# Latent attention: side weights' load and rounding written apart, O's second bank read by one copy, sums over keys in one VectorE instruction

## The chip, the core and the metric

The kernel runs on one NeuronCore of a Trainium2 chip. The metric is the device time of one execution in microseconds (us), the median of several runs. The five engines are called as the profile calls them: PE (TensorE, matmuls; PEld its weight loads), DVE (VectorE), ACT (ScalarE), POOL (GpSimd) and SP (SyncE, which here issues the DMAs). PE writes to PSUM, eight banks of 128 x 512 float32; DVE and ACT read PSUM, POOL works on SBUF alone.

## The reference, cut to what matters

Two layers run over 2048 latent tokens and 256 context tokens. The first layer mixes a windowed attention (mixer A) and a latent attention (mixer B); the second is a neighbourhood attention (mixer C). The change lies in mixer B's attention, and in the loading of the output weights beside mixers B and C. Mixer B has 8 heads; each latent query reads all 2304 keys, each context query the 256 context keys:

```python
def mla_dense(qn, qr, kn, kr, v):
    scale = (B_NOPE + B_ROPE) ** -0.5
    s = (jnp.einsum('bqhd,bkhd->bhqk', qn, kn) + jnp.einsum('bqhr,bkr->bhqk', qr, kr)).astype(jnp.float32) * scale
    p = jax.nn.softmax(s, axis=-1).astype(v.dtype)
    return jnp.einsum('bhqk,bkhd->bqhd', p, v)
...
    y = jnp.concatenate([oa * jax.nn.silu(za), ob * jax.nn.silu(zb)], axis=-1) @ out_w
```

## The kernel before, in words

**Numbers in two parts.** A float32 value x is kept as a high part (x rounded to the matmul's format) and a low part (x minus the high part). A product of two such values takes three matmuls, high x high, high x low and low x high. A weight tile is loaded into `ws` (L252), rounded on ACT into `wh` (L254), and the low part `wl` is made on POOL (L255); `wprep` does all three.

**Mixer B, `attn_b`.** The work of a head is cut into chunks of queries, 512 wide (256 wide for the context and for head 0's first two), in the order context, 0, 512, 1024, 1536. Inside a chunk the loop runs over 18 tiles of 128 keys (2 for the context). One step of it, `score(j)`, makes the scores of a key tile in PSUM (`bs`, three matmuls, L959 to L961), the exponential's high part (ACT, L964), the exponential in place (ACT, L965), the low part `bpl` (DVE, L966), and adds the high part into `bacc` (POOL, L970), which holds the sums over keys, one value for each partition and query. `pv(j)` comes four steps later (`LAG`) and adds two matmuls into two banks: `o` (L979, high part) and `o2` (L980, low part, 65 columns: 64 of the output and one of row sums). Both banks exist once (`op`, one buffer for each), so the next chunk's first `pv` writes to them when the last chunk's values have been read.

**The handover, `fin`.** After the last `pv` of a chunk, ACT copies `o` to `bos` (L984); DVE adds the 64 rows of `o2` to it (L986) and adds row 64 of `o2` into row 64 of `bacc` (L987). Two DMAs store `bos` (L989).

**The denominators, `den`.** Seven steps after `fin` (`DLAG`), PE transposes `bacc` by four blocks of 128 x 128 into one PSUM bank (L995), and ACT copies each block with an accumulator (L999), which sums over the keys. The bank (`xp`, one buffer) is shared with the transposes of row maxima (L935).

**The row maxima.** Between the steps of one chunk, the row maxima of the next one are made by a high x high matmul (`bm`, L923) and a maximum on DVE (L925); two banks.

**The side weights.** While mixer B runs, the first seven of eight row blocks of the output weights are prepared (`out_weights`, two `wprep` calls for each block, three `wst` buffers). In heads 1 to 7 one block is written ahead of the chunk that begins at 1024, under `tc.issue_after(self.vdma)`: what the block issues on SP stands behind the last DMA of the newest head load (`load(h + 1)`, written at chunk 512, some 4.7 MB). In mixer C (`attn_c`, 64 units of four row groups) three blocks are written, at units 19, 23 and 27, with no such order.

**What sets the order.** In `attn_b` PE runs in the order in which the program is written (`manual_schedule`). The orders of ACT, DVE, POOL and SP are made when the program is built, by a planner that plays the whole program through a timeline (`schedule_with_timeline_sim=True`): for each engine it takes, among the instructions whose inputs and buffers are ready in its timeline, the one written first. On the chip each engine then runs its list strictly in order, and waits on semaphores.

Of the kernel before, what the change touches and what calls it, by code (L numbers as in the profile page):

```python
# [8 lines left out]
F32 = mybir.dt.float32  # L9
R32 = mybir.dt.float32r  # L10
BF16 = mybir.dt.bfloat16
AF = mybir.ActivationFunctionType
ALU = mybir.AluOpType
AX = mybir.AxisListType
PSUM = bass.MemoryType.PSUM

P = 128
# [83 lines left out]
class Kern:  # L101
# [145 lines left out]

    def wprep(self, rings, sp, src, w, name, eng=None, bufs=3):

        nc = self.nc  # L250
        s = sp.tile([P, 512], F32, tag="wst", bufs=bufs, name="ws" + name)
        self.wdma = nc.sync.dma_start(s[:, :w], src).ins  # L252
        h, l = [r.tile([P, 512], R32, name=f"w{x}{name}") for x, r in zip("hl", rings)]
        nc.scalar.activation(h[:, :w], s[:, :w], AF.Copy)  # L254
        (eng or nc.gpsimd).tensor_sub(l[:, :w], s[:, :w], f(h[:, :w]))  # L255
        return h, l
# [580 lines left out]
    def out_weights(self, l, k0, k1, rings):  # L837
# [3 lines left out]
                                      512, f"o{l}{k}{hf}") for hf in range(2)])  # L841
        return [lambda k=k: go(k) for k in range(k0, k1)]

    def attn_b(self):


# [2 lines left out]
        nc, tc, i, scr = self.nc, self.tc, self.i, self.scr  # L849
        with ExitStack() as ctx:  # L850
# [96 lines left out]
            def st_pieces(h, t0, n):  # L947
                t = H[h]
                c = t0 // P
                kts = list(range(NT)) if t0 < TL else [NTL, NTL + 1]  # L950
                st = {}

                def score(j):
                    kt = kts[j]
                    if j == 0:
                        st["acc"] = p1.tile([P, 512], F32, tag="acc", bufs=3, name=f"bacc{h}_{c}")
                    ps = sp.tile([P, 512], F32, tag="s", name=f"bs{h}_{c}_{j}")
                    ks, qs = slice(kt * P, (kt + 1) * P), slice(t0, t0 + n)
                    nc.tensor.matmul(ps[:, :n], t["kh"][0:97, ks], t["qh"][0:97, qs], start=True, stop=False)  # L959
                    nc.tensor.matmul(ps[:, :n], t["kh"][0:96, ks], t["ql"][0:96, qs], start=False, stop=False)  # L960
                    nc.tensor.matmul(ps[:, :n], t["kl"][0:96, ks], t["qh"][0:96, qs], start=False, stop=True)  # L961
                    hi = ph.tile([P, 512], R32, name=f"bph{h}_{c}_{j}")
                    lo = pl_.tile([P, 512], R32, name=f"bpl{h}_{c}_{j}")
                    nc.scalar.activation(hi[:, :n], ps[:, :n], AF.Exp)  # L964
                    nc.scalar.activation(ps[:, :n], ps[:, :n], AF.Exp)  # L965
                    nc.vector.tensor_sub(lo[:, :n], ps[:, :n], f(hi[:, :n]))  # L966
                    if j == 0:
                        st["h0"] = hi
                    else:
                        nc.gpsimd.tensor_add(st["acc"][:, :n], f((st["h0"] if j == 1 else st["acc"])[:, :n]), f(hi[:, :n]))  # L970
                    st[j] = (hi, lo)

                def pv(j):
                    if j == 0:
                        st["o"] = op.tile([P, 512], F32, tag="o", name=f"bo{h}_{c}")
                        st["o2"] = op.tile([P, 512], F32, tag="o2", name=f"bo2{h}_{c}")
                    hi, lo = st.pop(j)
                    fi, la = j == 0, j == len(kts) - 1
                    nc.tensor.matmul(st["o"][:, :n], t["v"][:, kts[j], 0:P], hi[:, :n], start=fi, stop=la)  # L979
                    nc.tensor.matmul(st["o2"][0:65, :n], t["v"][:, kts[j], 64 : P + 1], lo[:, :n], start=fi, stop=la)  # L980

                def fin():
                    o = p.tile([P, 512], F32, tag="os", name=f"bos{h}_{c}")
                    nc.scalar.activation(o[:, :n], st["o"][:, :n], AF.Copy)  # L984
                    acc = st["acc"]
                    nc.vector.tensor_add(o[0:64, :n], st["o2"][0:64, :n], o[0:64, :n])  # L986
                    nc.vector.tensor_add(acc[64:65, :n], st["o2"][64:65, :n], acc[64:65, :n])  # L987
                    for e in range(2):
                        nc.sync.dma_start(scr["o0"][e, 512 + h * 64 : 576 + h * 64, t0 : t0 + n], o[e * 64 : e * 64 + 64, :n])  # L989

                def den():
                    d, c0 = den_of(h, t0)
                    ps = xp.tile([P, 512], F32, tag="x", name=f"bdt{h}_{c}")
                    for x in range(n // P):
                        nc.tensor.transpose(ps[:, x * P : (x + 1) * P], st["acc"][:, x * P : (x + 1) * P], self.ident)  # L995
                    for x in range(n // P):
                        col = t0 // P + x - c0
                        j = p.tile([P, P], BF16, tag="dj", bufs=1, name=f"bdj{h}_{c}_{x}")
                        nc.scalar.activation(j, ps[:, x * P : (x + 1) * P], AF.Copy, accum_out=d[:, col : col + 1])  # L999
                    late.put(8, lambda: den_done(h, t0, n))  # L1000

                k = range(len(kts))
                return [lambda j=j: score(j) for j in k], [lambda j=j: pv(j) for j in k], fin, den
# [5 lines left out]
            DLAG = 7  # L1009
            load(0)  # L1010

            side = self.out_weights(0, 0, self.nw, self.wor)
            late = Later()

            size = [sum(NT if t0 < TL else 2 for t0, _ in ch) for _, ch in units]
# [23 lines left out]
            for h, ch in units:  # L1039
                if ch[0][0] == 512 and h + 1 < 8:  # L1040
                    load(h + 1)
                if h > 0 and ch[0][0] == 1024 and side:
                    with tc.issue_after(self.vdma):
                        side.pop(0)()
                for x in ch:
                    score, pv, fin, den = st_pieces(h, *x)
                    for j in range(len(score)):
                        pvs.append(pv[j])
                        run(score[j], pvs.pop(0) if len(pvs) > LAG else None)
                    late.put(LAG, fin)  # L1050
                    late.put(LAG + DLAG, den)
# [301 lines left out]
    def attn_c(self):  # L1353
# [5 lines left out]
        with ExitStack() as ctx:  # L1359
# [163 lines left out]
            for n, (h, cb) in enumerate(units):  # L1523
                if cb == 2 and h + 1 < 16:
                    load(h + 1)
                if n + 3 < len(units):
                    load_v(*units[n + 3])
                if n + 1 < len(units):
                    make_bias(*units[n + 1])
                if n == 16:  # L1530
                    side = self.out_weights(1, 0, self.nw, self.wor)
                if n % 4 == 3 and side:
                    side.pop(0)()
                sl, Pt = s_pieces(h, cb)
                if len(queue) < 2:
                    merge(sl, [])
                else:
                    emit_t(sl)
                queue.append((h, cb, Pt))
# [122 lines left out]
```

## Time and profile before

| | us |
|---|---|
| median of 3 runs | 3759.67 (3757.97 to 3761.63) |
| the profiled execution | 3758.57 |
| its span, first to last instruction | 3756.8 |
| PE busy in the span | 3507.8 (93%) |
| DVE, ACT, POOL busy | 2311.3, 1945.0, 1668.9 |
| mixer B's loop, first to last score matmul | 961.8 to 1999.3 |
| mixer C's loop, the same | 3010.2 to 3524.8 |

The time of an execution is its span and some 1.8 us around it. In the profile each engine's instructions have a start and a length, and idle time ahead of an instruction is put down to what ended it. Matmuls overlap in the pipeline: at full speed those of 512 columns start 0.23 us apart though each is shown with 0.39 us. Neighbours on ACT, DVE and POOL overlap a little too, so that spacing is read from start to start. PEclk is the TensorE clock that was granted, as a share of 2.4 GHz: 1.00 or 0.50 (1.2 GHz).

### The profile page before, as it was taken

Reading aid. Unit: us, or ns where it says so; the run is one execution under the profiler, and the core shown is the slowest. Engines: PE = TensorE matmul, PEld = TensorE weight load, DVE = VectorE, ACT = ScalarE, POOL = GpSimd, SP = SyncE. Lnnn points to the kernel's source line nnn. Section 1 sums busy time; section 2 is a strip of 40 time slices with the busy share of each in tenths; the row PEclk is TensorE's granted clock in tenths of the full one; section 3 lists DMA queues with packets and bytes.
Section 4 is the critical chain, followed back from the end, with each engine's and each line's share of the span. In section 5 each row is a group of like instructions: output and inputs, shape, how many; then the busy total and the mean of one; then the engine's idle time right before and its main releaser. Section 6 shows DMA issues by size and latency. Waiting matters only on the chain.

```text
span 3756.8 us, 53300 instructions
## 1 busy us (share of the span) xinstructions
PE 3507.8 (93%) x17607; PEld 2889.5 (77%) x17607; DVE 2311.3 (62%) x4313; ACT 1945.0 (52%) x4096; POOL 1668.9 (44%) x1573
## 2 busy tenths in 40 slices
PE   6999899999989888988989989999999999999888
PEld 5777778889767666766767867888788789999766
DVE  6445542499978777877886874212211088888665
ACT  4343332599767666766763123223221188888511
POOL 6555642211567666766774244223211243333432
PEclk8999999999999999999989999999999999999999
DMA  6767563852321222023027956554434476666686
GB/s 216 222 205 242 183 176 119 278 130 57 70 67 23 53 66 67 9 67 75 22 65 223 318 195 190 169 145 126 136 129 127 149 278 243 236 240 232 190 225 177
DMA packets 381054, 576.79 MB, mean 154 GB/s; under 512 B 35393, under 2 KB 218081, under 8 KB 370913
## 3 DMA queue, kind: packets, MB, share of 16 engines
q1 hardware_dynamic: 380777, 573.39, 50.1%
q8 instruction: 138, 2.26, 0.2%
q14 instruction: 139, 1.14, 0.1%
HBM read 399.36 MB, written 173.90 MB: 153 GB/s over the span
## 4 chain that ended last, share of the span: by engine, by line
PE 66%; DMA 14%; DVE 7%; issue 5%; POOL 4%; ACT 3%; SPq 2%; POOLq 0%; ACTq 0%; DVEq 0%
PE mm L263 7%; PE mm L262 7%; PE mm L261 7%; PE co L650 4%; PE ptc L641 3%; PE bo L980 3%; PE bm L923 3%; PE bs L959 3%; PE bs L960 3%; PE bs L961 3%; DMA adat<-in_adat_dram 3%; PE bo L979 3%; PE ao L650 2%; DMA wso<-in_wo_dram 2%; DMA o<-s_rd 2%
## 5 line engine op out<-in xcount | busy, mean ns | idle before, releaser
L970 POOL TENSOR_TENSOR bacc<-bacc,bph 128x512 f32<-128x512 f32 (+1 forms) x528 | 667.2, 1264 | 192.9 <-ACT bph L964 164.5
L255 POOL TENSOR_TENSOR wl<-ws,wh 128x512 fp32r<-128x512 f32 (+2 forms) x320 | 425.3, 1344 | 650.8 <-ACT wh L254 579.2
L964 ACT ACTIVATE bph<-bs 128x512 fp32r<-128x512 f32 (+1 forms) x610 | 353.0, 579 | 254.3 <-PE bs L961 250.2
L925 DVE TENSOR_REDUCE bmx<-bm 128x1 f32<-128x512 f32 (+1 forms) x656 | 407.3, 629 | 108.7 <-PE bm L923 89.5
L966 DVE TENSOR_TENSOR bpl<-bs,bph 128x512 fp32r<-128x512 f32 (+1 forms) x610 | 402.3, 660 | 86.1 <-ACT bs L965 83.8
L965 ACT ACTIVATE bs<-bs 128x512 f32<-128x512 f32 (+1 forms) x610 | 351.9, 577 | 0.0
L254 ACT ACTIVATE wh<-ws 128x512 fp32r<-128x512 f32 (+2 forms) x328 | 197.5, 613 | 284.2 <-DMA ws<-in_w_dram 230.8
L261 PE MATMUL mm<-Uh,wh 128*128 128x512 f32 (+1 forms) x832 | 324.3, 390 | 0.4 <-ACT wh L254 0.4
L262 PE MATMUL mm<-Ul,wh 128*128 128x512 f32 (+1 forms) x832 | 323.8, 389 | 0.0
L263 PE MATMUL mm<-Uh,wl 128*128 128x512 f32 (+1 forms) x832 | 321.6, 389 | 0.4 <-POOL wl L255 0.4
L1431 POOL TENSOR_TENSOR cbias<-cbu,rm 128x384 f32<-128x384 f32 x144 | 158.0, 1112 | 343.5 <-DVE cnm L1459 216.5
L1459 DVE CUSTOM_DVE_ANT_0 cp<-cs,cbias 128x640 f32<-128x640 f32 (+1 forms) x256 | 222.2, 885 | 134.3 <-PE cs L1455 91.0
L980 PE MATMUL bo<-bpl,bv 128*65 128x512 f32 (+1 forms) x610 | 246.3, 404 | 53.9 <-DVE bacc L987 53.9
L959 PE MATMUL bs<-bqh,bkh 97*128 97x512 f32 (+1 forms) x610 | 250.6, 411 | 40.2 <-DVE bpl L966 39.3
L979 PE MATMUL bo<-bph,bv 128*128 128x512 f32 (+1 forms) x610 | 248.7, 408 | 14.3 <-ACT bos L984 14.3
L923 PE MATMUL bm<-bkh,bqh 96*128 96x512 f32 (+1 forms) x656 | 251.3, 398 | 3.6 <-DVE bmx L925 3.2
L240 DVE TENSOR_TENSOR plc<-ptc,phc 128x512 fp32r<-128x512 f32 (+1 forms) x384 | 235.1, 640 | 19.1 <-ACT phc L239 18.2
L960 PE MATMUL bs<-bql,bkh 96*128 96x512 f32 (+1 forms) x610 | 246.1, 403 | 0.0
L961 PE MATMUL bs<-bqh,bkl 96*128 96x512 f32 (+1 forms) x610 | 245.0, 402 | 0.0
L1464 ACT ACTIVATE cp<-cp,cnm 128x640 f32<-128x640 f32 (+1 forms) x256 | 226.1, 883 | 17.6 <-DVE cnm L1459 17.1
L239 ACT ACTIVATE phc<-ptc 128x512 fp32r<-128x512 f32 (+1 forms) x384 | 204.9, 558 | 55.6 <-PE ptc L641 55.1
L200 DVE SCALAR_TENSOR_TENSOR mj<-adat,scb 128x512 bf16<-128x512 f32 x144 | 120.1, 834 | 181.3 <-DMA adat<-in_adat_dram 169.1
(314 smaller groups left out, 8858.3 us busy)
## 6 DMA issues: line engine op xcount, KB each, us to landing
ws<-in_w_dram SPq DMA_DIRECT2D x256, 256.0 KB
ck<-s_kcT SPq DMA_DIRECT2D x32, 1152.0 KB
cv<-s_vc SPq DMA_DIRECT2D x64, 512.0 KB
adat<-in_adat_dram SPq DMA_DIRECT2D x96, 256.0 KB
o<-s_o SPq DMA_DIRECT2D x40, 512.0 KB
s_z<-zs SPq DMA_DIRECT2D x64, 256.0 KB
s_qcT<-st SPq DMA_DIRECT2D x64, 256.0 KB
s_kcT<-st SPq DMA_DIRECT2D x32, 512.0 KB
```

Source lines behind the costliest of these rows:

```text
L255: (eng or nc.gpsimd).tensor_sub(l[:, :w], s[:, :w], f(h[:, :w]))
L261: nc.tensor.matmul(out, a[0], b[0], start=first, stop=False)
L262: nc.tensor.matmul(out, a[0], b[1], start=False, stop=False)
L263: nc.tensor.matmul(out, a[1], b[0], start=False, stop=last)
L923: nc.tensor.matmul(ps[:, :w], t["qh"][0:96, b * P : (b + 1) * P], t["kh"][0:96, k0 : k0 + w], start=True, stop=True)
L925: nc.vector.tensor_reduce(t["mx"][:, j : j + 1], ps[:, :w], AX.X, ALU.max)
L959: nc.tensor.matmul(ps[:, :n], t["kh"][0:97, ks], t["qh"][0:97, qs], start=True, stop=False)
L960: nc.tensor.matmul(ps[:, :n], t["kh"][0:96, ks], t["ql"][0:96, qs], start=False, stop=False)
L966: nc.vector.tensor_sub(lo[:, :n], ps[:, :n], f(hi[:, :n]))
L970: nc.gpsimd.tensor_add(st["acc"][:, :n], f((st["h0"] if j == 1 else st["acc"])[:, :n]), f(hi[:, :n]))
L979: nc.tensor.matmul(st["o"][:, :n], t["v"][:, kts[j], 0:P], hi[:, :n], start=fi, stop=la)
L980: nc.tensor.matmul(st["o2"][0:65, :n], t["v"][:, kts[j], 64 : P + 1], lo[:, :n], start=fi, stop=la)
```

## The change

The rounding of side weights is written apart from their load: `wload` issues the DMA, `wsplit` does the ACT and POOL steps. In `attn_b` a block's load is written ahead of chunk 512 and its rounding ahead of chunk 1536 of the same head; in `attn_c` at units 17 and 19, 21 and 23, 25 and 27. In `fin`, DVE copies all 65 rows of `o2` into SBUF in one instruction, and POOL makes the two adds from there. In `den`, one DVE reduce over four blocks takes the place of the four ACT copies with accumulators.

```diff
@@ -247,9 +247,15 @@

     def wprep(self, rings, sp, src, w, name, eng=None, bufs=3):

+        return self.wsplit(rings, self.wload(sp, src, w, name, bufs), w, name, eng)
+
+    def wload(self, sp, src, w, name, bufs=3):
+        s = sp.tile([P, 512], F32, tag="wst", bufs=bufs, name="ws" + name)
+        self.wdma = self.nc.sync.dma_start(s[:, :w], src).ins
+        return s
+
+    def wsplit(self, rings, s, w, name, eng=None):
         nc = self.nc
-        s = sp.tile([P, 512], F32, tag="wst", bufs=bufs, name="ws" + name)
-        self.wdma = nc.sync.dma_start(s[:, :w], src).ins
         h, l = [r.tile([P, 512], R32, name=f"w{x}{name}") for x, r in zip("hl", rings)]
         nc.scalar.activation(h[:, :w], s[:, :w], AF.Copy)
         (eng or nc.gpsimd).tensor_sub(l[:, :w], s[:, :w], f(h[:, :w]))
@@ -841,6 +847,18 @@
                                       512, f"o{l}{k}{hf}") for hf in range(2)])
         return [lambda k=k: go(k) for k in range(k0, k1)]

+    def out_weights_apart(self, l, k0, k1, rings):
+
+        st = {}
+
+        def load(k):
+            st[k] = [self.wload(self.wop, self.i[f"wo{l}"][k * P : (k + 1) * P, hf * 512 : (hf + 1) * 512],
+                                512, f"o{l}{k}{hf}") for hf in range(2)]
+
+        def split(k):
+            self.W.append([self.wsplit(rings, s, 512, f"o{l}{k}{hf}") for hf, s in enumerate(st.pop(k))])
+        return [x for k in range(k0, k1) for x in (lambda k=k: load(k), lambda k=k: split(k))]
+
     def attn_b(self):


@@ -982,9 +1000,11 @@
                 def fin():
                     o = p.tile([P, 512], F32, tag="os", name=f"bos{h}_{c}")
                     nc.scalar.activation(o[:, :n], st["o"][:, :n], AF.Copy)
+                    o2 = p.tile([65, 512], F32, tag="os2", name=f"bos2{h}_{c}")
+                    nc.vector.tensor_copy(o2[:, :n], st["o2"][0:65, :n])
                     acc = st["acc"]
-                    nc.vector.tensor_add(o[0:64, :n], st["o2"][0:64, :n], o[0:64, :n])
-                    nc.vector.tensor_add(acc[64:65, :n], st["o2"][64:65, :n], acc[64:65, :n])
+                    nc.gpsimd.tensor_add(o[0:64, :n], o2[0:64, :n], o[0:64, :n])
+                    nc.gpsimd.tensor_add(acc[64:65, :n], o2[64:65, :n], acc[64:65, :n])
                     for e in range(2):
                         nc.sync.dma_start(scr["o0"][e, 512 + h * 64 : 576 + h * 64, t0 : t0 + n], o[e * 64 : e * 64 + 64, :n])

@@ -993,10 +1013,8 @@
                     ps = xp.tile([P, 512], F32, tag="x", name=f"bdt{h}_{c}")
                     for x in range(n // P):
                         nc.tensor.transpose(ps[:, x * P : (x + 1) * P], st["acc"][:, x * P : (x + 1) * P], self.ident)
-                    for x in range(n // P):
-                        col = t0 // P + x - c0
-                        j = p.tile([P, P], BF16, tag="dj", bufs=1, name=f"bdj{h}_{c}_{x}")
-                        nc.scalar.activation(j, ps[:, x * P : (x + 1) * P], AF.Copy, accum_out=d[:, col : col + 1])
+                    col = t0 // P - c0
+                    nc.vector.tensor_reduce(d[:, col : col + n // P], ps[:, :n].rearrange("p (t k) -> p t k", k=P), AX.X, ALU.add)
                     late.put(8, lambda: den_done(h, t0, n))

                 k = range(len(kts))
@@ -1009,7 +1027,7 @@
             DLAG = 7
             load(0)

-            side = self.out_weights(0, 0, self.nw, self.wor)
+            side = self.out_weights_apart(0, 0, self.nw, self.wor)
             late = Later()

             size = [sum(NT if t0 < TL else 2 for t0, _ in ch) for _, ch in units]
@@ -1039,7 +1057,7 @@
             for h, ch in units:
                 if ch[0][0] == 512 and h + 1 < 8:
                     load(h + 1)
-                if h > 0 and ch[0][0] == 1024 and side:
+                if h > 0 and ch[0][0] in (512, 1536) and side:
                     with tc.issue_after(self.vdma):
                         side.pop(0)()
                 for x in ch:
@@ -1528,8 +1546,8 @@
                 if n + 1 < len(units):
                     make_bias(*units[n + 1])
                 if n == 16:
-                    side = self.out_weights(1, 0, self.nw, self.wor)
-                if n % 4 == 3 and side:
+                    side = self.out_weights_apart(1, 0, self.nw, self.wor)
+                if n > 16 and n % 2 and side:
                     side.pop(0)()
                 sl, Pt = s_pieces(h, cb)
                 if len(queue) < 2:
```

## Rows read from the trace of the kernel before

**Rows 1.** The page: each engine's busy us (share of the span) and instructions.

```profile
PE 3507.8 (93%) x17607; PEld 2889.5 (77%) x17607; DVE 2311.3 (62%) x4313; ACT 1945.0 (52%) x4096; POOL 1668.9 (44%) x1573
```

**Rows 2.** Waits of PE from 960 to 2002: waiter, releaser, us, times, longest.

```profile
PE bo L980 <- DVE bacc L987: 53.9, 40, 4.5
PE bs L959 <- DVE bpl L966: 39.3, 9, 7.4
PE bo L979 <- ACT bos L984: 14.3, 37, 0.6
PE bdt L995 <- ACT bdj L999: 4.2, 3, 2.1
```

**Rows 3.** Timeline of PE at one handover: start, length, instruction, idle and releaser.

```profile
1161.74 0.39 PE L980 MATMUL bo<-bpl,bv 128*65 128x512 f32 x1
...
1162.69 0.40 PE L961 MATMUL bs<-bqh,bkl 96*128 96x512 f32 x1
1163.42 0.50 PE L979 MATMUL bo<-bph,bv 128*128 128x512 f32 x1 [0.34 <-ACT bos L984]
1165.16 0.42 PE L980 MATMUL bo<-bpl,bv 128*65 128x512 f32 x1 [1.23 <-DVE bacc L987]
```

**Rows 4.** Timeline of DVE, then of ACT, at the same handover.

```profile
1162.41 0.69 DVE L925 TENSOR_REDUCE bmx<-bm 128x1 f32<-128x512 f32 x1
1163.02 0.68 DVE L966 TENSOR_TENSOR bpl<-bs,bph 128x512 fp32r<-128x512 f32 x1
1163.62 0.67 DVE L986 TENSOR_TENSOR bos<-bo,bos 64x512 f32<-64x512 f32 x1
1164.32 0.69 DVE L987 TENSOR_TENSOR bacc<-bo,bacc 1x512 f32<-1x512 f32 x1
...
1162.78 0.59 ACT L984 ACTIVATE bos<-bo 128x512 f32<-128x512 f32 x1
```

**Rows 5.** Stretches: PE, PEld, DVE, ACT, POOL busy (instructions), PEclk, DMA, GB/s.

```profile
1040.00:1060.00 20.00, 20.00 (x94) 15.76 (x93) 18.47 (x34) 16.41 (x37) 16.02 (x13) 1.00 0.01 2
1160.00:1180.00 20.00, 18.43 (x85) 13.96 (x84) 17.78 (x32) 15.14 (x35) 15.90 (x13) 1.00 0.06 14
1214.00:1344.00 130.00, 114.79 (x488) 86.97 (x487) 102.95 (x186) 89.42 (x196) 90.50 (x72) 0.93 0.22 50
```

**Rows 6.** Same view, half-clock stretches, sums: 14 behind handovers, 6 behind side weights, head 7's 4.

```profile
sum 47.74, PE 47.62 PEld 34.98 DVE 21.07 ACT 18.35 POOL 15.95; mean PE 3.40 PEld 2.50 DVE 1.51 ACT 1.31 POOL 1.14
...
sum 58.03, PE 36.12 PEld 26.26 DVE 29.12 ACT 44.36 POOL 48.91; mean PE 6.02 PEld 4.38 DVE 4.85 ACT 7.39 POOL 8.15
...
sum 27.32, PE 21.30 PEld 15.82 DVE 16.15 ACT 9.00 POOL 13.52; mean PE 5.32 PEld 3.95 DVE 4.04 ACT 2.25 POOL 3.38
```

**Rows 7.** Timelines of SP, ACT and PE around head 1's side weights.

```profile
1094.08 10.05 SPq L252 DMA_DIRECT2D wso<-in_wo_dram  x2
...
1108.12 1.26 ACT L254 ACTIVATE who<-wso 128x512 fp32r<-128x512 f32 x2 [8.39 <-DMA wso<-in_wo_dram]
...
1111.13 0.80 PE L959 MATMUL bs<-bqh,bkh 97*128 97x512 f32 x1 [7.35 <-DVE bpl L966]
```

**Rows 8.** Two tiles from 3000 to 3545: length min/median/max, first and last start, form.

```profile
L254 ACT ACTIVATE who<-wso x6: 631/640/655, 3022.9 to 3036.5; 128x512 fp32r<-128x512 f32 x6
...
L1452 PE MATMUL cs<-ck,cq x256: 331/392/776, 3010.4 to 3524.8; 128*128 128x384 f32 x64, 128*128 128x512 f32 x64
```

**Rows 9.** Waits of PE, 1085 to 1100 (head 1's start), then 1900 to 2002 (head 7).

```profile
PE bo L980 <- DVE bacc L987: 2.1, 2, 1.3
...
PE bo L980 <- DVE bacc L987: 11.6, 3, 4.5
```

**Rows 10.** Groups of instructions from 960 to 2002: count, busy us, mean ns, idle.

```profile
L970 POOL TENSOR_TENSOR bacc<-bacc,bph 128x512 f32<-128x512 f32 x494 | 641.3, 1298 | 184.4 <-ACT bph L964 158.3 <-POOL bacc L970 0.8
L925 DVE TENSOR_REDUCE bmx<-bm 128x1 f32<-128x512 f32 x504 | 344.5, 688 | 99.9 <-PE bm L923 81.2
```

**Rows 11.** Timeline of POOL behind head 1's side weights: five adds back to back.

```profile
1111.27 6.72 POOL L970 TENSOR_TENSOR bacc<-bacc,bph 128x512 f32<-128x512 f32 x5
```

## The prediction

> **What bounds the kernel now.** I read the page first: PE is busy for 93% of the span [rows 1], so only PE's own idle and slow time can be saved, and the change touches mixer B, where I went next. The waits of PE there [rows 2] name four stalls. The largest, 53.9 us in 40 pieces, is the first `o2` matmul of a chunk waiting for L987. The second, 39.3 us, stands as 7.35 us behind head 1's side weights [rows 7], and alike in heads 2 to 6.
>
> The timeline of one handover [rows 3] shows how the first arises. The last matmul into `o2` starts at 1161.74. The next chunk's first L979 waits 0.34 us for ACT's copy, and its L980 starts 1.74 us after that (1165.16 less 1163.42), where neighbours stand 0.24 us apart (four steps from 1161.74 to 1162.69): 1.50 us late, of which 1.23 us is shown as idle. On DVE [rows 4] L986 can't begin before ACT's copy is done (1162.78 and 0.59 us), stands behind a `bpl`, and L987 follows. So `o2` is held through two DVE instructions that come late.
>
> A stall costs more than its idle time. Where PE just ran without one, its clock is 1.00 and it is busy throughout (first of [rows 5]). Behind 14 of the handovers the granted clock falls to 0.50 for 3.41 us with PE busy almost all the time: 47.62 us together, at 1.2 GHz (first sum of [rows 6]). Six stretches behind the side weights have 36.12 us of PE work at that clock, and four in head 7 have 21.30 us (the other sums of [rows 6]). Half of such work time is lost.
>
> **Part by part. The copy of `o2`.** Removed from DVE: L986 and L987, 0.67 and 0.69 us. Added: one copy out of PSUM of the same 512 columns; no row shows it at this size, so I bound it by 0 and by 0.69, and take 0.68, L986's, which also reads PSUM. It needs only PE's last matmul, not ACT. That ended near 1162.15 (1161.74 and about 0.4), and DVE began a maximum at 1162.41 and the `bpl` at 1163.02 [rows 4]. The copy is written before that maximum and is ready first, so the planner should put it there: done near 1163.0, before PE's L979 at 1163.42. L980 then finds its bank free, and the next thing late is L979's wait for ACT (14.3 us in all), which stays. What I gain:
>
> - L980's idle, 53.9 us. Two of the six handovers' pieces at each head's start, 2.1 us [rows 9], lie in heads 1 to 6 just ahead of the side weights' wait; PE would only arrive earlier at a DMA that lands no earlier. I leave 6 x 2.1 = 12.6 us out. Of head 7's 11.6 us in three pieces, where DVE also makes the output stage's sums, I take half. 53.9 - 12.6 - 5.8 = 35.5 us.
> - The restart, 1.50 - 1.23 = 0.27 us, at the other 28: 7.6 us.
> - The half clock. Twelve of the 14 stretches are not ahead of side weights: 47.62 / 2 x 12 / 14 = 20.4 us. Of head 7's 21.30 / 2, half: 5.3 us.
>
> **The two adds on POOL.** An add of 512 columns there takes 1.30 us [rows 10], 1.34 from start to start [rows 11]; no POOL row has fewer partitions, but on DVE 64 rows and 1 row cost alike [rows 4], so I take 1.34 for both, bounded by 0.69 (DVE's) and 2.6 (twice). POOL's load for a chunk becomes 17 x 1.34 and 2 x 1.34 = 25.5 us. PE's clean time for it is at least 18 steps of six matmuls at 0.24, 25.9 us. POOL is nearly full but not the bound; over head 2 it is busy for 90.5 us of 130 [rows 5], and gets about 12 more (eight adds and two of half width). Queued behind the adds are POOL's `bacc` adds, whose high parts have eight buffers, four steps of slack beyond `pv`; behind L989's stores on SP, which now wait for POOL, stands only the next head load, needed 100 us later. Cost taken: none, except at the end of mixer B, where the last sum waits for two POOL adds: 2.7 for 0.7, less what the reduce saves there, 1 us lost.
>
> **The reduce.** Four ACT copies with their accumulator reads go; one DVE reduce of 128 x 512 comes, 0.69 (L925 of [rows 10]). DVE's work at a handover stays at two instructions; it is 18.47 of 20 us busy where PE never waits [rows 5]. The bank it frees held PE up three times behind side weights, 4.2 us [rows 2]: gained.
>
> **The side weights.** I give this part nothing. The rounding that blocks ACT is written ahead of chunk 1024 of head 1, but ran at 1108, 14 us after its load was issued [rows 7] and early in that head's chunk 0 (the head began near 1085): the planner takes it as soon as its own timeline has the load landed. Mixer C shows it more plainly: blocks written at units 19 to 27 of 64 are rounded between 3022.9 and 3036.5, in a loop from 3010.4 to 3524.8 [rows 8], that is within units 2 to 5. The new code ties the rounding to nothing that comes later; `issue_after` orders SP alone, and the load has the same `vdma` ahead of it. So ACT still meets the rounding at the same point, with the exponentials queued behind it and PE behind those. Bounds: 0 and the 73 us of the second rival.
>
> **Sum.** 35.5 + 7.6 + 20.4 + 5.3 + 4.2 - 1.0 = 72.0 us off the profiled execution's 3758.6, which is its span and 1.8 us: 3686.6. The median lies 1.1 us higher: 3687.7, called 3688.
>
> **Rivals.** *The copy stands late.* If DVE's list has it where L986 is, it ends at 1164.3: 0.70 us saved of 1.50. 28 x 0.70 = 19.6, half of the slow-clock terms 12.8, and 3.2 of the rest: 36 us, 3723. For it: the list is made in another timeline than the chip's. Against it: the copy is ready before two instructions that L986 wasn't. Chance 0.15.
>
> *The side weights' wait goes too.* Then 39.3 us of idle, 36.12 / 2 of slow clock, and the 12.6 and 3.4 left out: 73 us more, 3615. For it: as written, two chunks now lie between load and rounding. Against it: one chunk and more lay ahead of the rounding as written before, and rows 7 and 8 show the planner passing over such distances. Chance 0.07.
>
> *The half clock stays.* L979's wait for ACT remains at every handover; if it alone brings the clock down, 25.7 us are not gained: 3713. Against it: the stretch at 1160 holds 0.34 and 1.23 us of idle and keeps 1.00 [rows 3, 5]. The Trainium skill ("TensorE: Matmul & The Clock Gate", A second HAM failure mode: psum-queue depth-cycling) has short idle times between groups of matmuls, from cycling PSUM banks, make the clock swing; by that rule this rival is what comes, the trace so far shows it only behind both waits together. Chance 0.10.
>
> *Slower: POOL's backlog reaches PE.* PE runs its list in order, and seven steps, 7 x 1.44 = 10.1 us, after the handover come the transposes of `bacc`, which now wait for POOL's second add. One add under way and two new ones take 4.0 us, so a backlog B of POOL costs B - 6.1 us at each of 41 handovers. It eats the gain of 72 us at B = 7.9 and shows as slower just above. At 9 us: 41 x 2.9 = 119, less 72: 3807. For it: five adds in a row behind side weights [rows 11]. Against it: POOL is 16.02 of 20 us busy at PE's full pace [rows 5], so such a backlog shrinks. The Trainium skill ("GPSIMD Engine Reference", Engine selection) says to keep two-input adds on VectorE, GpSimd being about half as fast; 1.30 against 0.67 agrees, and the rule decides only if POOL is on the path. Chance 0.05.
>
> *The parts cancel* (a new order elsewhere gives the gain back): 3760. Chance 0.03.
>
> **How the numbers follow.** The forecast has 0.60. Its own range: all terms whole give 53.9 + 10.8 + 23.8 + 10.7 + 4.2 = 103 us, 3656; the late copy is its upper neighbour, 3723. The range 3655 to 3728 holds the forecast, the late copy and the half clock but for their tails, about 0.8; outside are 0.07 below and 0.08 above. A measurement here can tell about 0.2%, 7.5 us, from no change. Faster by more: 0.60 + 0.15 + 0.10 + 0.07 = 0.92; within: 0.03; slower: 0.05.
>
> **What would show it.** Right: among PE's waits L980 no longer waits for DVE (under 5 us), L979 still waits some 14 us for ACT, the 3.41 us stretches at 0.50 behind handovers are gone, and PE still waits near 39 us behind the side weights, six times. Wrong: L980 waiting for the copy's line (late copy); L254 without a wait for its DMA (second rival); L995 waiting for POOL (slower).

## The result: 3670 us, 0.976 of the time before

The kernel after takes 3670.2 us (median, 3666.0 to 3674.0) against 3758.8; the ratio is 0.9764, interval 0.9747 to 0.978, 88.6 us less. The prediction was 3688, with 3655 to 3728 as its range. The profiled executions differ by 92.0 us of span (3756.8 and 3664.8). That run of after is the one read here. Its lines stand 18 or 20 further down than before's: L959 is L977, L980 is L998, L984 is L1002, L995 is L1015; the rounding L254 is L260.

The page of after, engine rows (busy us, share of the span, instructions), to be read against [rows 1]:

```profile
PE 3474.2 (95%) x17607; PEld 2871.1 (78%) x17607; DVE 2293.3 (63%) x4313; ACT 1904.1 (52%) x3808; POOL 1759.3 (48%) x1655
```

PE does the same 17607 matmuls in 33.6 us less: part of the gain is clock, not idle time. DVE has as many instructions as before, POOL 82 more and ACT 288 fewer.

**Where the time went.** I measure mixer B from ACT's first copy of `o` to its last: 967.96 to 2002.62 before, 967.98 to 1914.23 after. It is 88.4 us shorter, and all that lies behind it 3.6. The windows of just these stretches, before and then after (PE, PEld, DVE, ACT, POOL busy and count, PEclk, DMA share, GB/s):

```profile
967.96:2002.62 1034.66, 919.20 (x3956) 697.84 (x3955) 835.87 (x1511) 721.37 (x1591) 737.74 (x593) 0.93 0.21 52
...
967.98:1914.23 946.25, 884.08 (x3955) 677.92 (x3954) 810.26 (x1508) 681.63 (x1310) 819.35 (x667) 0.97 0.24 56
```

PE's idle time falls from 115.5 to 62.2 us (length less busy), 53.3 of the 88.4; the other 35.1 us are busy time of the same matmuls. The time spent at a granted clock of 0.50 falls from 139.9 to 61.4 us, and PE's work within it from 111.4 to 45.7. At that clock matmuls of 512 columns start 0.43 us apart (1951.19 to 1951.62 in before), at full clock 0.235, so 45% of such work is lost: 29.6 of the 35.1 us. The rest I put down to waiting that is shown as busy: a matmul is shown 0.39 us long, so the first 0.16 us or so of a wait behind it leave no idle time. PE's waits in that stretch of after (waiter, releaser, us, times, longest), which answer to [rows 2]:

```profile
PE bs L977 <- DVE bpl L984: 42.2, 14, 6.9
PE bo L997 <- ACT bos L1002: 15.2, 38, 0.8
PE bm L941 <- DVE bmx L943: 3.4, 4, 1.6
...
PE bo L998 <- DVE bos L1004: 0.2, 1, 0.2
```

The second bank's wait, 53.9 us in 40 pieces, is down to 0.2 us; the wait for ACT's copy is what it was; the transposes' wait for ACT is gone; the wait behind the side weights is there. One handover, PE, then DVE, ACT and POOL (start, length, instruction, idle ahead and its releaser), which answers to [rows 3] and [rows 4]:

```profile
1148.10 0.39 PE L998 MATMUL bo<-bpl,bv 128*65 128x512 f32 x1
...
1149.78 0.50 PE L997 MATMUL bo<-bph,bv 128*128 128x512 f32 x1 [0.34 <-ACT bos L1002]
1150.12 0.40 PE L998 MATMUL bo<-bpl,bv 128*65 128x512 f32 x1
...
1148.60 0.69 DVE L1004 COPY bos<-bo 65x512 f32<-65x512 f32 x1
1149.20 0.68 DVE L943 TENSOR_REDUCE bmx<-bm 128x1 f32<-128x512 f32 x1
...
1149.13 0.59 ACT L1002 ACTIVATE bos<-bo 128x512 f32<-128x512 f32 x1
...
1150.97 1.29 POOL L1006 TENSOR_TENSOR bos<-bos,bos 64x512 f32<-64x512 f32 x1
1152.23 1.28 POOL L988 TENSOR_TENSOR bacc<-bacc,bph 128x512 f32<-128x512 f32 x1
1153.60 1.29 POOL L1007 TENSOR_TENSOR bacc<-bos,bacc 1x512 f32<-1x512 f32 x1
```

The copy starts 0.50 us after the start of the bank's last matmul and ends at 1149.29, half a microsecond before L997 starts; L998 follows 0.34 us behind it, where it stood 1.74 before.

At head 1's side weights ([rows 7] before), SP's first issue of that burst and the first one of the side weights, ACT's rounding and PE's stall:

```profile
1077.33 0.46 SPq L894 DMA_DIRECT2D bkh<-s_kbT  x1
...
1086.81 9.40 SPq L254 DMA_DIRECT2D wso<-in_wo_dram  x1
...
1102.18 1.29 ACT L260 ACTIVATE who<-wso 128x512 fp32r<-128x512 f32 x2 [8.10 <-DMA wso<-in_wo_dram]
...
1105.23 0.79 PE L977 MATMUL bs<-bqh,bkh 97*128 97x512 f32 x1 [6.91 <-DVE bpl L984]
```

ACT waits 8.10 us for the weights, 8.39 before. Writing the rounding a chunk later left it where it was.

### The profile page after: what moved, and what is told of

Same layout as the page of the kernel before. It is cut to its first block, busy times and chain, and to the rows that moved or that the text cites. A ratio compares the mean times of both kernels' runs of the same rounds, so it can differ in the third digit from the quotient of the medians.

```text
span 3664.8 us, 52981 instructions
## 1 busy us (share of the span) xinstructions
PE 3474.2 (95%) x17607; PEld 2871.1 (78%) x17607; DVE 2293.3 (63%) x4313; ACT 1904.1 (52%) x3808; POOL 1759.3 (48%) x1655
## 5 line engine op out<-in xcount | busy, mean ns | idle before, releaser
L984 DVE TENSOR_TENSOR bpl<-bs,bph 128x512 fp32r<-128x512 f32 (+1 forms) x610 | 401.3, 659 | 59.4 <-ACT bs L983 58.1
L260 ACT ACTIVATE wh<-ws 128x512 fp32r<-128x512 f32 (+2 forms) x328 | 197.1, 613 | 266.6 <-DMA ws<-in_w_dram 211.2
L977 PE MATMUL bs<-bqh,bkh 97*128 97x512 f32 (+1 forms) x610 | 246.6, 404 | 42.9 <-DVE bpl L984 42.2
L997 PE MATMUL bo<-bph,bv 128*128 128x512 f32 (+1 forms) x610 | 242.3, 397 | 15.4 <-ACT bos L1002 15.2
L240 DVE TENSOR_TENSOR plc<-ptc,phc 128x512 fp32r<-128x512 f32 (+1 forms) x384 | 235.3, 640 | 18.1 <-ACT phc L239 17.3
L979 PE MATMUL bs<-bqh,bkl 96*128 96x512 f32 (+1 forms) x610 | 239.0, 392 | 0.0
L998 PE MATMUL bo<-bpl,bv 128*65 128x512 f32 (+1 forms) x610 | 238.0, 390 | 0.4 <-DVE bpl L984 0.2
L1482 ACT ACTIVATE cp<-cp,cnm 128x640 f32<-128x640 f32 (+1 forms) x256 | 226.3, 884 | 17.6 <-DVE cnm L1477 17.4
```

## The experiments

Lengths below come from the times between ACT's copies of `o`; idle is PE's in that stretch, half the time with a granted clock of 0.50 (idle time in it included), all in us. The names of the runs stand at the results below. "Six stretches" are those of heads 1 to 6 from the copy of the last head's last chunk, over the narrow chunk, to the copy of chunk 0; the side weights' stall lies in them.

```
                mixer B              six stretches
                length idle  half    length idle  half
before          1034.7 115.5 139.9   260.8  60.1  71.7
fin_only         956.5  77.4  68.3   250.1  60.4  64.9
reduce_only     1018.4 108.2 109.2   248.2  52.8  51.2
no_side_split    948.2  64.2  64.9   232.5  41.7  54.6
after            946.2  62.2  61.4   231.2  41.2  47.8
late_round       895.9  30.1  13.7   180.7   5.3   0.0
late_swap        892.8  21.7  10.2   181.1   2.9   0.0
load_first       953.5  68.8  75.1   231.2  40.8  51.2
adds_dve         995.0  84.1  81.9   232.2  33.4  51.2
fin_heads       1024.4 115.7 136.5   249.0  59.4  68.3
pool2            991.4  98.4  92.2   254.7  62.1  58.0
pool4           1053.2 130.9 150.2   248.9  54.3  64.9
```

### One part alone: the handover

To the kernel before, only this was done:

```diff
+                    o2 = p.tile([65, 512], F32, tag="os2", name=f"bos2{h}_{c}")
+                    nc.vector.tensor_copy(o2[:, :n], st["o2"][0:65, :n])
-                    nc.vector.tensor_add(o[0:64, :n], st["o2"][0:64, :n], o[0:64, :n])
-                    nc.vector.tensor_add(acc[64:65, :n], st["o2"][64:65, :n], acc[64:65, :n])
+                    nc.gpsimd.tensor_add(o[0:64, :n], o2[0:64, :n], o[0:64, :n])
+                    nc.gpsimd.tensor_add(acc[64:65, :n], o2[64:65, :n], acc[64:65, :n])
```

> The kernel before with one part of the change: at a chunk's end O's second bank is read by one DVE copy, and the two adds on POOL. Denominators and side weights stay as they were. Theory A (this part carries nearly all of the gain: L980's 53.9 us of idle and the slow clock behind the handovers, with the head starts' pieces gained as well): 3671 to 3684 us, PE's wait for the second bank under 2 us in all, the bdt transposes still waiting 3 to 6 us for ACT. Theory B (the reduce's four freed ACT copies a chunk carry a third of it): 3695 to 3710 us. Theory C (the step of the prediction as written, the head starts held back at their DMA): about 3692 us.

Measured (fin_only): 3684.4 us, ratio 0.9806 (0.978 to 0.9832), 73 us less. The interval, 3675 to 3694 us, holds most of theory A's range and C's 3692, so the time does not tell these two apart; B is out. The trace sides with C on the idle time, which stays at 60.4 us in the six stretches (60.1 before), and it shows why the run stays short of after. PE's waits in mixer B:

```profile
PE bdt L997 <- POOL bacc L970: 45.4, 5, 10.0
PE bo L979 <- ACT bos L984: 15.3, 39, 0.6
PE bdt L997 <- ACT bdj L1001: 10.0, 1, 10.0
...
PE bo L980 <- DVE bos L986: 0.4, 1, 0.4
```

The second bank's wait is gone (0.4), but behind the side weights PE now stops earlier, at the transposes of the denominators, for 55.4 us in six pieces instead of 39.3 and 4.2. POOL is named as the releaser of five. ACT's list, with PE's restart, shows who held them:

```profile
1103.34 0.63 ACT L254 ACTIVATE who<-wso 128x512 fp32r<-128x512 f32 x1 [6.51 <-DMA wso<-in_wo_dram]
1103.87 0.26 ACT L1001 ACTIVATE bdj<-bdt 128x128 bf16<-128x128 f32 x1
...
1107.46 0.19 ACT L1001 ACTIVATION_READ_ACCUMULATOR bdj<-bdt 128x1 f32 x1
...
1107.80 0.66 PE L997 MATMUL bdt<-ident,bacc 128*128 128x128 f32 x2 [8.57 <-POOL bacc L970]
```

The one transposes' bank is emptied by ACT's copies L1001, which stand behind the blocked rounding; the last ends at 1107.65 and PE starts at 1107.80. At all six stalls PE starts 0.14 us after the last L1001. At the sixth, the one that names ACT, POOL's add had ended 0.56 us before, so POOL is not what PE waits for there.

### One part alone: the reduce

```diff
-                    for x in range(n // P):
...
-                        nc.scalar.activation(j, ps[:, x * P : (x + 1) * P], AF.Copy, accum_out=d[:, col : col + 1])
+                    nc.vector.tensor_reduce(d[:, col : col + n // P], ps[:, :n].rearrange("p (t k) -> p t k", k=P), AX.X, ALU.add)
```

> The kernel before with one part of the change: the sums over keys by one DVE reduce of 128 x 512 in place of four ACT copies with accumulator reads. Theory A: only the bdt transposes' wait goes, 4.2 us, less what a third DVE instruction per chunk costs where the second bank is still read by two DVE adds: 3752 to 3760 us. Theory B (ACT freed at the handovers): 3725 to 3740 us, with L979's 14.3 us of wait for ACT down by a third or more.

Measured (reduce_only): 3745.4 us, 0.9968 (0.9953 to 0.9984), 12 us less, between the two. L979's wait stays at 14.6 us, so ACT freed at the handovers is not the reason and B is out. The six stretches give 12.6 us, of which 7.3 are idle time (60.1 to 52.8) and 5.3 PE's busy time: its work at half clock there falls from 49.2 to 38.1 us, and 45% of that difference is 5.0.

### The side weights' part undone

The kernel after, with load and rounding written together at chunk 1024 as before:

> The kernel after with the side weights' part undone (load and rounding written together at chunk 1024, as before). Theory A (that part does nothing, the roundings run where they ran): 3666 to 3676 us, ACT's wait for wso 6 to 9 us at each of the heads 1 to 6, as after. Theory B (the part contributes): over 3680 us, and longer waits of PE behind the side weights than after's 5 to 7 us.

Measured (no_side_split): 3672.9 us, 0.9777 (0.9751 to 0.9803), indistinguishable from after's 0.9764; theory A. The side weights' part of the change does nothing that these runs can tell (their intervals leave room for some 10 us). In mixer C of after it is the same: of a loop that runs from 2921.3 to 3436.0, the six roundings take place in the first 25 us again, as in the first 27 before ([rows 8]):

```profile
L1470 PE MATMUL cs<-ck,cq x256: 331/393/796, 2921.3 to 3436.0; 128*128 128x384 f32 x64, 128*128 128x512 f32 x64
...
L260 ACT ACTIVATE who<-wso x6: 624/639/662, 2933.7 to 2945.5; 128x512 fp32r<-128x512 f32 x6
```

### The rounding tied late

To the kernel after, one ordering edge. `issue_after` orders what a block issues on the engine of the instruction it is given; with ACT's last exponential in place of an SP transfer it orders ACT:

```diff
-                    nc.scalar.activation(ps[:, :n], ps[:, :n], AF.Exp)
+                    self.bexp = nc.scalar.activation(ps[:, :n], ps[:, :n], AF.Exp).ins
...
-                    with tc.issue_after(self.vdma):
+                    with tc.issue_after(self.vdma if ch[0][0] == 512 else self.bexp):
                         side.pop(0)()
```

> The kernel after with one ordering edge more in mixer B: the rounding of the side weights is queued on ACT behind the last exponential written ahead of it (end of chunk 1024). Theory A (ACT's list held the rounding early; tied late it finds its weights landed): PE's six waits of 36 us in all go, and half of the 55 us at half clock that follow them: 3600 to 3618 us, ACT's L260 without a wait for wso. Theory B (the wait only moves: another transfer or POOL's subtraction is late next): 3640 to 3672 us.

Measured (late_round): 3616.6 us, 0.963 (0.960 to 0.966), theory A: 54 us below after and the fastest version here but for a tie below. The rounding's line, of after up to 1700 and then of this kernel up to 1760 (ACT's L260; what ended its idle time, us, times):

```profile
L260 ACT ACTIVATE who<-wso x14: 612/629/631, 1102.2 to 1698.5; 128x512 fp32r<-128x512 f32 x14
its engine sat idle before it (us, times) until:
  DMA wso<-in_wo_dram: 43.3, 6
...
L260 ACT ACTIVATE who<-wso x12: 615/617/620, 1166.4 to 1716.7; 128x512 fp32r<-128x512 f32 x12
its engine sat idle before it (us, times) until:
who waited for it (us, times):
```

The list is empty in the second: the rounding begins at 1166.4 and nothing is waited for; the later ones, up to 1900.6, wait for nothing either. The six stretches fall from 231.2 to 180.7 us, their idle from 41.2 to 5.3 and their time at half clock from 47.8 to nothing. PE still waits 15.8 us for ACT's copies in 40 pieces, and mixer B has half clock for 13.7 us only, all of it in head 7 (from 1845.5).

### SP's order turned around

```diff
                 if h > 0 and ch[0][0] in (512, 1536) and side:
                     with tc.issue_after(self.vdma):
                         side.pop(0)()
+                if ch[0][0] == 512 and h + 1 < 8:
+                    with tc.issue_after(self.wdma):
+                        load(h + 1)
```

> The kernel after with SP's order turned around: the side weights' two loads are issued ahead of the next head's ten loads, which wait for them; the rounding on ACT stays where its planner puts it. Theory A (the rounding waits because the side weights' transfer stands behind 5.8 MB of head loads): they land some us after their issue, ACT's wait for wso falls under 10 us in all, 3600 to 3625 us. Theory B (the rounding is planned right at the load's landing, wherever that is): ACT still waits at six heads, 3645 to 3672 us.

Measured (load_first): 3684.5 us, 0.9812 (0.9788 to 0.9837); B's direction, but beyond its range, and the edit didn't do what I meant. SP's list around head 1:

```profile
1089.65 0.46 SPq L894 DMA_DIRECT2D bkh<-s_kbT  x1
...
1097.62 0.38 SPq L901 DMA_DIRECT2D bv<-s_vb  x1
1099.05 9.85 SPq L254 DMA_DIRECT2D wso<-in_wo_dram  x2
```

The side weights still stand right behind ten head loads, now those of the head before in the program's order. The burst starts near the end of the head before, as in after (1077.33 there), and the side weights land behind it. ACT's six waits for `wso` are 43.3 us again: the rounding moved with its load. So the run does not test whether an early landing would do; it shows once more that the planner puts the rounding at the load. Why it is 14 us slower than after stays open; the six stretches are the same, and the rest of mixer B is 7.3 us longer.

### The adds back on DVE

The kernel after with `nc.vector` for `nc.gpsimd` in the two adds of `fin`, still from SBUF:

> The kernel after with the two adds of a chunk's end on DVE instead of POOL (from SBUF; O's second bank is still read by the copy alone). Theory A (what holds PE up is the bank, and DVE has room for 1.4 us more in 26.9): 3664 to 3680 us, PE without a wait for the second bank. Theory B (DVE is too full at a handover, the adds delay the bpl's that PE's next steps need): 3690 to 3730 us, with PE waiting for bpl behind the handovers.

Measured (adds_dve): 3712.6 us, 0.9876 (0.9857 to 0.9895), theory B's time: 42 us slower than after, though PE waits more for the row maxima and the copy than for `bpl`. PE's waits, and the stretch 1142 to 1169 of this kernel and then of after:

```profile
PE bm L941 <- DVE bmx L943: 27.4, 26, 1.9
PE bs L977 <- DVE bpl L984: 19.1, 10, 5.4
PE bo L997 <- ACT bos L1002: 15.3, 39, 0.8
PE bo L998 <- DVE bos L1004: 15.3, 9, 2.2
...
1142.00:1169.00 27.00, 25.40 (x113) 19.09 (x112) 25.22 (x43) 19.12 (x36) 19.64 (x17) 1.00 0.05 11
...
1142.00:1169.00 27.00, 26.66 (x121) 20.55 (x120) 25.09 (x46) 20.55 (x39) 24.51 (x20) 1.00 0.05 10
```

DVE is busy for 25 us of 27 in both, but PE gets 113 matmuls done instead of 121, and waits for the row maxima, for `bpl` and for the copy itself. With the adds on DVE the change shortens mixer B by 39.6 us; the other 48.8 of its 88.4 need them off DVE.

The expectation priced the two adds at 1.4 us for a chunk, by [rows 4], where one input of each is in PSUM. With both inputs in SBUF the wide ones take more than twice as long on DVE (count, busy us, mean ns, in mixer B of this kernel):

```profile
L1006 DVE TENSOR_TENSOR bos<-bos,bos 64x512 f32<-64x512 f32 x30 | 46.6, 1554 | 0.8
L1007 DVE TENSOR_TENSOR bacc<-bos,bacc 1x512 f32<-1x512 f32 x30 | 41.9, 1396 | 0.9
```

Of the 62 wide adds in the whole run 48 take 1.2 to 1.8 us and the rest 0.67 to 0.69. The two that have no POOL instruction beside them are short, and so are 12 that have one. `bpl`, with one input in PSUM, stays at 0.65 to 0.69 us in all 558 cases, 525 of them beside POOL. So the long ones are adds out of SBUF beside a working POOL; what sorts long from short there is not shown. On POOL, in after, the two adds take 1.32 and 1.28 us.

The Trainium skill ("GPSIMD Engine Reference", Engine selection) keeps elementwise adds on VectorE, GpSimd being about half as fast with two inputs. The trace agrees for adds with an input in PSUM (0.67 in [rows 4] against 1.29 on POOL); for these, out of SBUF, it does not, and the time speaks for POOL too.

### The handover at the heads' starts alone

The kernel before, with the new `fin` under a condition, the old one elsewhere:

```diff
+                    if (h < 6 and t0 == 1536) or (0 < h < 7 and n < 512):
```

> The kernel before with the new handover (copy, adds on POOL) only at the starts of heads 1 to 6: the last chunk of heads 0 to 5 and the narrow chunk of heads 1 to 6. Theory A (the prediction's step: PE only arrives earlier at the side weights' DMA): no change, 3750 to 3760 us on the scale of a before of 3758. Theory B (the DMA is issued when the head before releases its buffers, so it moves with PE and all is gained): 12.6 us of idle, 3.2 of restart, 3.4 of slow clock, 19 us less: 3735 to 3743.

Measured (fin_heads): 3738.7 us, 0.9948 (0.9931 to 0.9966): 13 to 26 us less, theory B's size. Its trace does not bear out B's reason. The waits for the second bank fall by 12.2 (53.9 to 41.7), and those behind the side weights rise from 43.5 to 55.4:

```profile
PE bdt L1001 <- POOL bacc L970: 44.5, 5, 9.6
PE bo L980 <- DVE bacc L993: 41.7, 28, 4.5
...
PE bdt L1001 <- ACT bdj L1005: 10.0, 1, 10.0
PE bs L959 <- DVE bpl L966: 0.9, 4, 0.3
```

Idle time in mixer B is 115.7 against 115.5: what was saved ahead of the weights was waited for behind them, as theory A has it. Yet the six stretches are 11.8 us shorter, 11.1 of it PE's busy time. The time at half clock falls by 3.4 us only, but PE's work in it falls from 49.2 to 30.5 us: the longer wait takes up more of the slow stretches. 45% of that difference is 8.4 us, which with the 3.2 expected for the restarts is the busy time within 0.5. So A is right about the idle time and not about the time, and B's size comes from the clock and not from the load.

### More work on POOL

The kernel after with two, or four, adds more ahead of the two real ones:

```diff
+                    for _ in range(2):
+                        xx = p.tile([65, 512], F32, tag="xx", bufs=1, name=f"bxx{h}_{c}")
+                        nc.gpsimd.tensor_add(xx[:, :n], o2[:, :n], o2[:, :n])
```

> The kernel after with two adds more on POOL at every chunk's end, ahead of the two real ones; their result isn't used. POOL is busy for 101.3 us of head 2's 118 in the kernel after; two adds of 1.35 us at four chunks and of 0.75 at the narrow one make 113.9. Theory A (as the slower rival has it: a backlog costs PE nothing up to 6.1 us, and the time per head is enough): 3668 to 3690 us. Theory B (POOL's adds lie on the path already): 12.6 us a head, 3765 to 3790 us.

> As pool2, with four adds more: 126 us of POOL's work for a head of 118, 31 us for a chunk of 26.9. Theory A (POOL becomes the bound, by 8 us a head at least, by 16 if it can't use the time in which PE waits for the side weights): 3730 to 3800 us, with PE or ACT waiting for POOL's bacc. Theory C (the eight buffers of high parts and the steps ahead of the transposes absorb it): under 3690 us.

Measured: two more (pool2) 3714.1 us, 0.9875 (0.9843 to 0.9907), between A and B; four more (pool4) 3803.1 us, 1.0118 (1.0081 to 1.0154), A but for 3 us, slower than the kernel before. With two more, POOL is not full (108 us of 120 busy in the stretch from 1280), and still PE loses 44 us. Its list behind head 2's side weights, with PE's stall, says how for the largest part:

```profile
1236.04 1.26 POOL L261 TENSOR_TENSOR wlo<-wso,who 128x512 fp32r<-128x512 f32 x1 [5.75 <-ACT who L260]
1237.26 1.26 POOL L988 TENSOR_TENSOR bacc<-bacc,bph 128x512 f32<-128x512 f32 x1
1238.48 1.27 POOL L261 TENSOR_TENSOR wlo<-wso,who 128x512 fp32r<-128x512 f32 x1
1239.83 1.25 POOL L1010 TENSOR_TENSOR bacc<-bos,bacc 1x512 f32<-1x512 f32 x1
...
1241.14 1.11 PE L1018 MATMUL bdt<-ident,bacc 128*128 128x128 f32 x4 [12.55 <-POOL bacc L1010]
```

The handover's second add (L1010) now stands behind the side weights' subtraction, which waits for the rounding, which waits for its DMA; PE's transposes wait 12.55 us for it. Such waits are 46.9 us in all, 40.8 of them in the six stretches, while PE's wait for `bpl` falls from 42.2 to 18.1. The six stretches give 23.5 of the 45.1 us by which mixer B is longer than in after. Another 14.3 are its last chunk (23.24 to 37.53), where PE waits for `bpl`; that part stays open. The slower rival's path is real, and it opens by order in POOL's list before POOL is full.

### A chunk's first step turned around

late_round, with the matmul into `o2` ahead of the one into `o` where j is 0:

> late_round with the two matmuls of a chunk's first PV step in the other order: the one into the second bank first, the one into the first bank, which waits for ACT's copy, 0.24 us later. Theory A (L997's wait of about 0.34 us is due to when ACT's copy ends, and the second bank is free by then): the wait for ACT falls from 15.8 to 4 to 8 us, 3605 to 3612 us. Theory B (PE only comes to wait for the second bank's copy on DVE in its place): 3613 to 3622 us, with a wait for the copy's line of some 8 us or more.

Measured (late_swap): 3618.8 us, 0.9624 (0.9604 to 0.9645), no difference from late_round that the runs can tell; the profiled execution, 3609.6, was the fastest of four. The wait for ACT's copy falls from 15.8 to 0.4 us, as theory A says, and mixer B's idle time by 8.5. But PE is busy for 871.2 us instead of 865.8, and the length of mixer B falls by 3.1 only. Part of the wait is still there, shown as busy. Counted from start to start against the normal spacing, an estimate from the trace's start times, the waits at the two banks fall by 9.0 us (27.8 to 18.8); 2.5 come back at the matmuls for the row maxima, 2.5 at the transposes and 1.0 at the scores. So A is right that the banks' waits fall and wrong that the gain stays; B's wait for the copy is 4.8 us and not 8, and the rest is lost elsewhere.

## Why the prediction was right, and where its steps were not

**What bounded the kernel: right.** All of the gain but 3.6 us lies in mixer B, and the second bank's wait, named first, went from 53.9 to 0.2.

**The copy of `o2`: right, by its own times.** Forecast: ahead of the maximum that follows the bank's last matmul, done before PE's L979, lasting about 0.68. Measured: just there, 0.69. The late copy is out: L998 waits for the copy's line for 0.2 us.

**The slow clock: right in size where it was forecast; the restart too high.** Forecast 20.4 + 5.3 for the clock and 7.6 for the restart, 33.3, all outside the six stretches. PE's busy time in mixer B fell by 35.1, but 10.7 of that lie in the six stretches; elsewhere it fell by 24.4. PE's work at half clock fell there from 62.2 to 13.1 us, and 45% of that is 22 (the prediction took half of such work as lost), near the 25.7 for the clock. Some 2 us are left beside the restart's 7.6. The rival that the half clock stays is out: L997's wait for ACT, 38 pieces, is as it was (15.2 us against 14.3), and around such a handover the clock is 1.00 (1142 to 1169, above). So the wait that stayed doesn't lower the clock by itself. The Trainium skill's sentence on short idle times between groups of matmuls ("TensorE: Matmul & The Clock Gate", A second HAM failure mode: psum-queue depth-cycling) speaks of a bf16 kernel and is not borne out here for waits of 0.34 us once in a chunk; late_round shows it best, with 40 of them and 13.7 us at half clock in 896.

**Held back at the head starts: the step that failed.** Forecast: 12.6 us of idle and two slow stretches not gained, the six stretches giving only the reduce's 4.2. Measured: 29.6. The mechanism is half right. The load does come a fixed time after the head's end, 17.4 to 18.8 us from the last chunk's copy to the rounding in heads 1 to 6, before as after; and with the handover alone the idle time was indeed waited for again (60.4 us in fin_only's six stretches, 60.1 before). Two things were missed. One is the clock: even with the handover alone less of PE's work falls at half clock there (30.8 us against 49.2), and the stretches are 10.7 us shorter. The other is that the transposes' bank was the next thing to stop PE, held by ACT's copies behind the rounding. With the handover ACT has done nine of chunk 0's score steps ahead of the rounding, in fin_only as in after, where it had done six or seven before; but only with the reduce on DVE does PE run on to use them. Of the 60.4 us, 41.7 are left in no_side_split, and the stretches are 28.3 us shorter, against 10.7 and 12.6 for the two parts alone.

**The reduce: mis-sized.** Priced at the 4.2 us of waits that the trace showed under its own name; worth 12 alone, and another 11.5 beside the handover (3684.4 to 3672.9).

**The other handovers: too high by 10.** Forecast 68.8 us for idle, restart and clock away from the side weights; measured 88.4 - 29.6 = 58.8. The idle time came as forecast (34.4 us, 35.5 forecast); the busy time fell short (24.4 against 33.3). Of the missing 10.0, 6.6 are one chunk of head 6: from copy to copy 33.28 us in after and 26.69 in fin_only. There ACT's exponentials wait for POOL, some 20 us after four roundings of side weights in 5 us. fin_only has the same four and no such loss, and in after POOL sits idle for 3.3 us shortly before (to 1711.91), so a backlog left by the roundings is not shown to be the cause; it stays open (ACT at that place, after):

```profile
1716.98 0.60 ACT L982 ACTIVATE bph<-bs 128x512 fp32r<-128x512 f32 x1 [1.21 <-POOL bacc L988]
...
1720.70 0.60 ACT L982 ACTIVATE bph<-bs 128x512 fp32r<-128x512 f32 x1 [2.64 <-POOL bacc L988]
```

**The adds on POOL: cost right, margin wrong.** Durations 1.29, for 64 rows and for one, against 1.34 taken. No wait of PE for POOL's `bacc` stands among after's, so "none" held, but for head 6. The margin was put at 6.1 us of backlog; two more adds, 2.6 us, already cost 44 (3714.1 against 3670.2). And that the adds, once out of SBUF, would cost DVE 3.0 us for a chunk was not among my reasons; adds_dve shows that nearly half of the gain hangs on having them elsewhere.

**The tail: wrong sign, by little.** Forecast 1.0 us lost; all behind the last copy is 3.6 shorter. The last sum does wait, but on DVE:

```profile
1943.30 0.37 PE L677 MATMUL dnb<-ident,denb 128*4 128x128 f32 x1 [8.35 <-DVE denb L675]
```

**The side weights: right.** Nothing was given, nothing came; no_side_split and the rounding's unchanged place show it. The second rival, that the wait goes too, was priced at 73 us. Done in earnest by late_round it brings 54 (3670.2 to 3616.6; 50.4 between the profiled executions): the six stretches give 50.5, head 6's chunk 6.6 (33.28 to 26.70), and the last chunk of head 7 gives 8.6 back (23.24 to 31.88).

**In sum:** 4.2 against 29.6 in the six stretches, 68.8 against 58.8 elsewhere in mixer B, -1.0 against 3.6 behind it: 72.0 forecast, 92.0 measured between the profiled executions. That the median came within 18 us of the forecast is partly luck, since a step that was too careful and one that was too bold cancel in part. The range did not need it: with either error alone the sum is 102.0 or 66.6 us, 3658 or 3693.

## What to carry to other kernels

Writing an instruction later in the program does not make it run later where a planner sorts the lists; if an instruction waits for a DMA, tie it on its own engine behind work that outlasts the transfer, and look in the trace whether its engine still sits idle ahead of it. When a stall is removed, look for the next single buffer on the same path and for what empties it: two parts that free neighbouring buffers are worth more in the stretch where both bind than the two show alone (28.3 us against 10.7 and 12.6 here). Take an instruction's price for the operands that it will have: the adds cost DVE 0.67 us with an input in PSUM, and 1.4 to 1.55 on average out of SBUF beside a busy POOL. Moving an instruction off the engine that is late can pay, but it brings the other engine's in-order queue with it, with every wait in that queue.

## What the runs showed of the hardware

POOL's add goes by columns and not by partitions: 1.29 us for 64 x 512 as for 1 x 512. DVE's add with both inputs in SBUF took up to 1.8 us at 512 columns beside a working POOL (48 of 62), 0.68 without; with an input in PSUM it kept to 0.69. DVE's copy of 65 x 512 from PSUM takes 0.685 us, about as long as its reduce of 128 x 512 to 128 x 4 (0.69), which replaces four ACT copies of 0.277 and four accumulator reads of 0.199, 1.9 us of durations in all. And a busy share did not show how late an engine was: at 25.2 of 27 us DVE held PE up, at 25.1 it did not.
